# Differential attention's score products: 32-row fp32 matmuls replaced by one pass over stacked high and low parts

## The chip, the cores and the metric

The kernel runs on one core of one Trainium2 chip. The metric is the device time of one execution in microseconds (us), from the first to the last instruction with what lies around them; lower is better. The core has a matrix engine (PE, with its weight loads listed apart as PEld), a vector engine (DVE), a scalar engine (ACT), GpSimd (POOL) and SyncE (SP), which issues most of the DMAs. Each engine works through its own queue in order and waits on semaphores for the others.

## The reference

Two layers of an encoder for 256 tokens of width 1024. Each layer has token mixing (three head groups side by side), cross-attention into 256 memory tokens, and a gated feed-forward part with a short convolution. The change touches group C of the mixing, differential attention with 4 heads, each with two pairs of queries and keys of 32 values:

```python
def diff_group(dq, dk, dv, lam, lam_init, g_sub, cos, sin):
    q = partial_rope(dq.reshape(b, s, DIFF_HEADS, 2, DIFF_QK_DIM), cos, sin, 2 * DIFF_ROT)
    k = partial_rope(dk.reshape(b, s, DIFF_HEADS, 2, DIFF_QK_DIM), cos, sin, 2 * DIFF_ROT)
    v = dv.reshape(b, s, DIFF_HEADS, DIFF_V_DIM)
    scale = DIFF_QK_DIM ** -0.5
    def block(qb):
        sc = jnp.einsum('bqhcd,bkhcd->bhcqk', qb, k).astype(jnp.float32) * scale
        p = jax.nn.softmax(sc, axis=-1)
        a = (p[:, :, 0] - lam * p[:, :, 1]).astype(v.dtype)
        return jnp.einsum('bhqk,bkhe->bqhe', a, v)
```

So there are 8 score products per layer (4 heads by 2), each of 256 queries by 256 keys over 32 values.

## The kernel before

All large products are made with split operands: a float32 matrix is cut into a high part in the type fp32r, written by ACT, and a low part, the remainder, written by DVE (function `split`, lines 139 and 140; for weights with a gain lines 262 and 263). A product is then three fp32r matmuls, high by high, high by low and low by high (`mm_nat`, lines 270, 272 and 274; `mm_T`, lines 277 to 279). Weights stream in through `wunit`: a DMA into one of 6 raw buffers, then the split into one of 6 pairs. Plain float32 matmuls are used for transposes, for attention weights times values, and for the scores of the mixing groups (lines 638 and 770).

The mixing stage of a layer is a list of short steps written by hand (`MIX`, one string per layer). A step traces its instructions; a planner then orders the queue of each engine by the place in the trace and by what is ready, with costs of its own, so that instructions of neighbouring steps are interleaved. Only SyncE's queue stands as written.

The steps that matter here: `dL` and `dM0`/`dM1` make the projection for queries and keys of group C. `dn0`/`dn1` (`diff_qk`) copy one block of 128 tokens out of PSUM with its row factor on ACT and rotate it on DVE. `dT0`/`dT1` (`diff_qk_T`) transpose the block on PE and copy it to the tile `dT`, queries and keys apart, both on ACT. `s0` to `s3` (`diff_scores`) make the scores of a head, two PSUM banks of 2 blocks each, and call `softmax_exp` (row maximum on DVE, line 471; exponentials on ACT, line 475). `t` turns the probabilities, `w` multiplies them with the values. Around them stand `vL`/`vM` (values of group C, weights of 256 columns), `uL`/`wL`, `q`, `Q`, `kv`, `K`, `a`, `b`, `v`, `o` (group A), `zu`, `zv`, `sgu`, `ws`, `sg` (group B), `ms`, `mf`, `mg` (normalising, transposing and scaling the memory tokens, layer 0 only), and `pl`/`p`, pieces of the memory's keys and values that run in the single PSUM bank `fil`.

A score product before is two matmuls, one for each block of queries, on 32 of the 128 rows of PE's array; `tile_position` picks which rows. DVE's `rstd` chains pass through POOL (lines 159 and 178). The pool `t4` has 16 buffers of 4 KB a partition; `dT` takes one.

Of the kernel before, what the change touches and what calls it, by code (L numbers as in the profile page):

```python
# [13 lines left out]
F32 = mybir.dt.float32  # L14
F32R = mybir.dt.float32r
I32 = mybir.dt.int32
AF = mybir.ActivationFunctionType
ALU = mybir.AluOpType
# [3 lines left out]
P = 128  # L22
D = 1024
S = 256
# [11 lines left out]
H_C, QK_C, V_C, ROT_C = 4, 32, 64, 16  # L36
# [14 lines left out]

MIX = (
# [7 lines left out]
MEM = (  # L60
# [5 lines left out]
    "uL cw uM0 e0 uM1 e1")  # L66
BUFS = {"t4": 16, "t2": 10, "raw": 6, "w": 6, "acc": 4, "att": 3, "fil": 1, "gB": 2}

ENG = {"mrow": "A", "mT": "V", "dval": "A", "dn": "A", "dTq": "A", "dTk": "A", "kT": "A", "kn": "V",
    "va": "A", "qn": "A", "qT": "A", "mq": "A", "mo": "V", "up": "A", "ws": "A", "pt": "A"}  # L70
BANK = {"pd": "att", "po0": "acc", "po1": "acc", "tp": "att", "sc": "acc", "xs": "att", "xo": "att"}

# [2 lines left out]
def encoder(ctx, tc, a, out):  # L75
    nc = tc.nc
    V, A_, G, T = nc.vector, nc.scalar, nc.gpsimd, nc.tensor
# [9 lines left out]
    def nm(s):  # L87
        uid[0] += 1
        return f"{s}_{uid[0]}"

    def t4(dt=F32):
        return act.tile([P, UNIT], dt, tag="t4", bufs=BUFS["t4"], name=nm("t4"))

    def t2(dt=F32):
        return act.tile([P, 512], dt, tag="t2", bufs=BUFS["t2"], name=nm("t2"))
# [4 lines left out]
    def psum1(tag="att"):  # L100
        return pp.tile([P, 512], F32, tag=tag, bufs=BUFS[tag], name=nm(tag))

    def small(n, tag, bufs=4):
        return sm.tile([P, n], F32, tag=tag, bufs=bufs, name=nm(tag))
# [12 lines left out]
    mT = const.tile([P, KD, S], F32, name="mT")  # L117
# [20 lines left out]
    def split(h, lo, src):  # L138
        return (A_.activation(h, src, AF.Copy),  # L139
                V.tensor_tensor(lo, src, h.bitcast(F32), op=ALU.subtract))  # L140

    def copy(at, dst, src, scale=None):
        if ENG[at] == "A":
            A_.activation(dst, src, AF.Copy, scale=1.0 if scale is None else scale)
        elif scale is None:
            V.tensor_copy(dst, src)
        else:
            V.tensor_scalar(dst, src, scale, None, op0=ALU.mult)
# [94 lines left out]
    def group_T(src, kt):  # L243
        ps = psum1()
        pv = ps.rearrange("p (k b t) -> p k b t", k=2, b=NB)
        for b in range(NB):
            for k in range(2):
                T.transpose(pv[:, k, b, :], src[:, b, blk(k)], ident)
        split(hTH[:, kt:kt + 2, :], hTL[:, kt:kt + 2, :], ps.rearrange("p (k t) -> p k t", k=2))
# [31 lines left out]
    def blk(b):  # L281
        return slice(b * P, (b + 1) * P)
# [83 lines left out]
    def rope(out_v, src, n, rot, cs, sn):  # L366
        hf = rot // 2
        ta = sm.tile([P, 256], F32, tag="ropeA", bufs=1, name=nm("ropeA"))[:, :n * rot].rearrange("p (n r) -> p n r", r=rot)
        tb = sm.tile([P, 256], F32, tag="ropeB", bufs=1, name=nm("ropeB"))[:, :n * rot].rearrange("p (n r) -> p n r", r=rot)
        V.tensor_tensor(ta, src, cs.unsqueeze(1).broadcast_to([P, n, rot]), op=ALU.mult)  # L370
        V.tensor_tensor(tb[:, :, :hf], src[:, :, hf:], sn[:, :hf].unsqueeze(1).broadcast_to([P, n, hf]), op=ALU.mult)
        V.tensor_tensor(tb[:, :, hf:], src[:, :, :hf], sn[:, hf:].unsqueeze(1).broadcast_to([P, n, hf]), op=ALU.mult)  # L372
        V.tensor_tensor(out_v, ta, tb, op=ALU.add)
# [94 lines left out]
    def softmax_exp(acc):  # L468
        sv = acc.rearrange("p (b k) -> p b k", b=NB)
        nmx = small(NB, "nmax", 4)  # L470
        V.tensor_reduce(nmx, sv, axis=AX.X, op=ALU.max, negate=True)
        e = t2().rearrange("p (b k) -> p b k", k=S)
        ssum = small(NB, "psum", 10)
        for b in range(NB):
            A_.activation(e[:, b, :], sv[:, b, :], AF.Exp, bias=nmx[:, b:b + 1], accum_out=ssum[:, b:b + 1])
        return e, ssum
# [33 lines left out]
    for l in range(DEPTH):  # L510
# [3 lines left out]
        if l == 0:  # L514
# [5 lines left out]
            rr = []  # L520
        gm = pre_cols[:, l * KD:(l + 1) * KD]

        st = SimpleNamespace(units={}, e={}, t={}, flip={}, kr=[None] * NB, qn=[None] * NB, kn=[None] * NB)
        steps = mem.steps()
# [81 lines left out]

        def diff_qk(b):
            st.dn[b] = dn = t2()
            copy("dn", dn, st.d[b], rr[b])
            dv_ = dn.rearrange("p (n d) -> p n d", d=QK_C)  # L610
            rope(dv_[:, :, :ROT_C], dv_[:, :, :ROT_C], 16, ROT_C, cosD[:, b, :], sinD[:, b, :])

        def diff_qk_T(b):
            if b == 0:
                st.dT = t4().rearrange("p (k t) -> p k t", t=S)
            ps = psum1()
            for i in range(4):
                T.transpose(ps[:, blk(i)], st.dn[b][:, blk(i)], ident)
            pv = ps.rearrange("p (k t) -> p k t", t=P)
            copy("dTq", st.dT[:, 0:2, blk(b)], pv[:, 0:2, :], QK_C ** -0.5)  # L620
            copy("dTk", st.dT[:, 2:4, blk(b)], pv[:, 2:4, :])

        def diff_values():
            steps["vM_"]()
# [4 lines left out]
        def diff_scores(h):  # L629
            if h == 0:  # L630
                st.sd = small(NB * H_C, "s0s", 3).rearrange("p (b h) -> p b h", b=NB)
            es = []
            for c in range(2):
                acc = psum1(BANK["sc"])
                g = 2 * h + c
                rows = slice((g % 4) * QK_C, (g % 4 + 1) * QK_C)
                for b in range(NB):
                    T.matmul(acc[:, b * S:(b + 1) * S], st.dT[rows, g // 4, blk(b)], st.dT[rows, 2 + g // 4, :],  # L638
                             start=True, stop=True, tile_position=((g % 4) * QK_C, 0))
                es.append(softmax_exp(acc))  # L640
            (e0, s0), (e1, s1) = es
            V.tensor_copy(st.sd[:, :, h], s0)
            cf = small(NB, "cf", 2)
            V.reciprocal(cf, s1)
            V.scalar_tensor_tensor(cf, cf, nlam, s0, op0=ALU.mult, op1=ALU.mult)
            for b in range(NB):
                V.scalar_tensor_tensor(e0[:, b, :], e1[:, b, :], cf[:, b:b + 1], e0[:, b, :], op0=ALU.mult, op1=ALU.add)
            st.e["d", h] = e0
# [27 lines left out]
                V.tensor_tensor(ov, ov, st.gsc.unsqueeze(1).broadcast_to([P, H_C, V_C]), op=ALU.mult)  # L676

        steps["vM_"] = steps["vM"]
        steps.update(vM=diff_values, do=diff_out, gd=lambda: group_T(st.oc.rearrange("p b h d -> p b (h d)"), 6))
        for b in range(NB):  # L680
            steps[f"dn{b}"] = partial(diff_qk, b)
            steps[f"dT{b}"] = partial(diff_qk_T, b)
        for h in range(H_C):
            steps[f"s{h}"] = partial(diff_scores, h)
            steps[f"t{h}"] = partial(turn, ("d", h))
            steps[f"w{h}"] = partial(diff_v, h)
# [132 lines left out]
        rr = []  # L819
# [7 lines left out]
        steps = {"pl": mem.piece_load, "p": mem.piece}  # L827
        if l + 1 < DEPTH:
            steps = {**mems[l + 1].steps(), **steps}
# [67 lines left out]
        steps = mems[l + 1].steps() if l + 1 < DEPTH else {}  # L897
# [28 lines left out]
        for j in range(0, NF, 2):  # L926
# [4 lines left out]
            for s_ in range(2):  # L931
                if j < 4 and s_ == 0:
                    srcs = [first[j // 2][:, m * S:(m + 1) * S] for m in range(2)]
                else:
# [5 lines left out]
                    for m, acc in enumerate(accs()):  # L940
                        for kt in range(KD):
                            wH, wL = us[kt // 4]
# [16 lines left out]
        rr = [] if l + 1 < DEPTH else None  # L959
# [26 lines left out]
```

## Time and profile before

| what | value |
|---|---|
| time, median of 3 runs | 851.68 us (850.91 to 852.28) |
| profiled execution, its own time | 851.3 us |
| its span, first to last instruction | 849.5 us |
| PE busy | 833.2 us, 98% |
| DVE busy | 625.5 us, 74% |
| ACT busy | 546.9 us, 64% |
| POOL busy | 39.1 us, 5% |
| mean granted clock of PE | 0.997 of full speed |

The busy time of PE counts matmuls whose pipelines overlap, so the duration of one instruction is longer than the distance to the next one. What an instruction costs PE is read from the distance between starts. The chain of waits lists exactly that: each piece there lasts until the next piece of the chain takes over.

### The profile page before, as it was taken

To read this page: it belongs to the slowest core of one execution; us is meant where nothing else is said; L and a number is where in the kernel's file an instruction comes from. 1 tells how busy PE (TensorE), PEld (TensorE's weight loads), DVE (VectorE), ACT (ScalarE), POOL (GpSimd) and SP (SyncE) were. 2 spreads that over 40 slices of the span, in tenths; PEclk is the share of its full clock that TensorE was granted. 3 is DMA by queue.
4 is the path that set the end of the run, shared out by engine and by line. 5 is a ranking of instruction groups with operands and counts; after the bars stand their busy time and mean duration, and the time that the engine had idled before them with its cause. 6 is when DMAs were issued, how large, how long until landed. Compare 5 with 4: busy or idle time off the path is not lost.

```text
span 849.5 us, 13117 instructions
## 1 busy us (share of the span) xinstructions
PE 833.2 (98%) x4846; PEld 728.4 (86%) x4846; DVE 625.5 (74%) x1127; ACT 546.9 (64%) x1027; POOL 39.1 (5%) x65
## 2 busy tenths in 40 slices
PE   7999999999999999999999999999998999999997
PEld 5898999889888888888889989988996888888885
DVE  6798664776488999974487787548566799999543
ACT  7798663766368777763376777547636587777331
POOL 1120000100020000000010100001001000000000
PEclk9999999999999999999999999999999999999999
DMA  7873533572355667655737723256624446775531
GB/s 276 275 228 104 166 100 100 156 251 90 94 160 173 201 208 212 203 173 193 219 116 216 236 82 124 76 148 219 191 62 148 154 148 199 223 218 184 183 109 50
DMA packets 94704, 141.64 MB, mean 167 GB/s; under 512 B 5806, under 2 KB 71172, under 8 KB 94640
## 3 DMA queue, kind: packets, MB, share of 16 engines
q1 hardware_dynamic: 94368, 140.59, 52.8%
q8 instruction: 38, 0.62, 0.3%
q14 instruction: 26, 0.21, 0.1%
q0 software_dynamic: 160, 0.18, 0.1%
q10 hardware_dynamic: 112, 0.03, 0.0%
HBM read 139.74 MB, written 1.05 MB: 166 GB/s over the span
## 4 chain that ended last, share of the span: by engine, by line
PE 91%; DVE 4%; POOL 1%; issue 1%; DMA 1%; ACT 1%; SPq 0%; DVEq 0%; POOLq 0%; ACTq 0%
PE acc L943 18%; PE acc L270 13%; PE acc L272 13%; PE acc L274 13%; PE acc L944 9%; PE fil L270 2%; PE fil L274 2%; PE fil L272 2%; PE fil L277 2%; PE att L484 2%; PE fil L278 2%; PE fil L279 2%; PE acc L770 2%; PE acc L782 2%; PE acc L638 1%; PE att L204 1%
## 5 line engine op out<-in xcount | busy, mean ns | idle before, releaser
L140 DVE TENSOR_TENSOR wl<-raw,wh 128x1024 fp32r<-128x1024 f32 (+1 forms) x206 | 249.7, 1215 | 119.9 <-ACT wh L139 118.2
L139 ACT ACTIVATE wh<-raw 128x1024 fp32r<-128x1024 f32 (+1 forms) x206 | 215.6, 1051 | 129.6 <-PE acc L274 85.8
L943 PE MATMUL acc<-hT,wh 128*128 128x512 f32 x640 | 224.3, 396 | 0.0
L944 PE MATMUL acc<-hT,wl 128*128 128x256 f32 x640 | 178.8, 279 | 0.0
L943 PEld LDWEIGHTS acc<-hT,wh 128*128 128x128 f32 x640 | 120.2, 188 | 28.7
L272 PE MATMUL acc<-wl,hT 128*128 128x512 f32 (+3 forms) x384 | 134.9, 373 | 0.0
L274 PE MATMUL acc<-wh,hT 128*128 128x512 f32 (+3 forms) x384 | 134.4, 372 | 0.3 <-DVE hT L140 0.3
L270 PE MATMUL acc<-wh,hT 128*128 128x512 f32 (+3 forms) x384 | 134.7, 375 | 0.0
L944 PEld LDWEIGHTS acc<-hT,wl 128*128 128x128 f32 x640 | 120.7, 189 | 0.0
L274 PEld LDWEIGHTS acc<-wh,hT 128*128 128x128 f32 x384 | 72.7, 190 | 12.2 <-DVE hT L140 1.4
L272 PEld LDWEIGHTS acc<-wl,hT 128*128 128x128 f32 x384 | 72.6, 190 | 11.8 <-DVE wl L140 0.7
L270 PEld LDWEIGHTS acc<-wh,hT 128*128 128x128 f32 x384 | 72.3, 190 | 11.4 <-ACT hT L139 0.4
L270 PE MATMUL acc<-wh,t 128*128 128x512 f32 (+1 forms) x216 | 67.7, 387 | 0.0
L272 PE MATMUL acc<-wl,t 128*128 128x512 f32 (+1 forms) x216 | 67.5, 386 | 0.0
L274 PE MATMUL acc<-wh,t 128*128 128x512 f32 (+1 forms) x216 | 67.0, 384 | 0.0
L950 ACT ACTIVATE t<-t,cw 128x256 f32<-128x256 f32 x80 | 47.5, 595 | 13.9 <-DVE t L946 13.4
L262 ACT ACTIVATE wh<-raw,pre_cols 128x512 fp32r<-128x512 f32 (+3 forms) x80 | 43.7, 616 | 11.9 <-PE acc L274 7.8
L263 DVE SCALAR_TENSOR_TENSOR wl<-raw,pre_cols,wh 128x512 fp32r<-128x512 f32 (+3 forms) x80 | 46.1, 621 | 4.5 <-ACT wh L262 4.5
L270 PEld LDWEIGHTS acc<-wh,t 128*128 128x128 f32 x216 | 39.9, 188 | 8.2 <-issue 0.7
L274 PEld LDWEIGHTS acc<-wh,t 128*128 128x128 f32 x216 | 40.4, 188 | 7.5
L272 PEld LDWEIGHTS acc<-wl,t 128*128 128x128 f32 x216 | 40.3, 188 | 7.6 <-DVE ropeB L372 0.3
L178 POOL TENSOR_TENSOR rstd<-ms,nhalf 128x1 f32<-128x1 f32 x18 | 14.7, 819 | 605.0 <-DVE ms L176 600.4
(189 smaller groups left out, 1397.8 us busy)
## 6 DMA issues: line engine op xcount, KB each, us to landing
raw<-in_ffn_w_up SPq DMA_DIRECT2D x88, 512.0 KB, 4.6
raw<-in_ffn_w_down SPq DMA_DIRECT2D x44, 512.0 KB, 3.4
raw<-in_mem_w_kv SPq DMA_DIRECT2D x32, 512.0 KB, 3.7
raw<-in_w_in SPq DMA_DIRECT2D x20, 512.0 KB, 4.8
raw<-in_w_mix_out SPq DMA_DIRECT2D x16, 512.0 KB, 3.4
raw<-in_mem_w_q SPq DMA_DIRECT2D x16, 512.0 KB, 3.9
raw<-in_mem_w_o SPq DMA_DIRECT2D x16, 512.0 KB, 4.3
raw<-in_w_in SPq DMA_DIRECT2D x8, 384.0 KB, 4.6
```

The costliest lines, as they stand in the source:

```text
L139: return (A_.activation(h, src, AF.Copy), V.tensor_tensor(lo, src, h.bitcast(F32), op=ALU.subtract))
L140: V.tensor_tensor(lo, src, h.bitcast(F32), op=ALU.subtract))
L262: A_.activation(h[:, v], raw[:, v], AF.Copy, scale=g[:, i:i + 1])
L263: V.scalar_tensor_tensor(lo[:, v], raw[:, v], g[:, i:i + 1], h[:, v].bitcast(F32), op0=ALU.mult, op1=ALU.subtract)
L270: T.matmul(o, sH, w, start=start, stop=False)
L272: T.matmul(o, sH, w, start=False, stop=False)
L274: T.matmul(o, sL, w, start=False, stop=stop)
L277: T.matmul(o, wH, sH, start=start, stop=False)
L278: T.matmul(o, wH, sL, start=False, stop=False)
L943: T.matmul(acc, wH[:, kt % 4, blk(m)], hT[:, kt, :, :], start=kt == 0, stop=False)
L944: T.matmul(acc[:, :S], wL[:, kt % 4, blk(m)], hTH[:, kt, :], start=False, stop=kt == KD - 1)
L950: A_.activation(cv[:, m, :], src, AF.Identity, bias=cw[:, 3, f:f + 1], scale=cw[:, 1, f:f + 1])
```

## The change

Queries and keys of group C are cut into high (H) and low (L) parts and stacked: for each of the 8 score products, 96 rows hold H, H, L of the queries and H, L, H of the keys. One fp32r matmul over 96 rows then gives HH + HL + LH. The stacking copies between partitions are a step of their own, `dS`, placed right behind `dT1` in both lists. The scale of the queries moves into `diff_qk`.

```diff
-    "dT1 vL ms0 ms1 kF1 vM mf0 mf1 kF0 mg0 uL s0 q0 sg s1 q1 Q0 mg1 wL kv0 p s3 t0 Q1 w0 t1 pl s2 kv1 pg K0 "
+    "dT1 dS vL ms0 ms1 kF1 vM mf0 mf1 kF0 mg0 uL s0 q0 sg s1 q1 Q0 mg1 wL kv0 p s3 t0 Q1 w0 t1 pl s2 kv1 pg K0 "
-    "dL con dM0 dn0 zL dM1 zM cL cM dn1 pl kL dT0 p zu zv sgu dT1 ws cn0 vL cn1 kM cF0 kn0 uL kn1 vM sg kF0 "
+    "dL con dM0 dn0 zL dM1 zM cL cM dn1 pl kL dT0 p zu zv sgu dT1 dS ws cn0 vL cn1 kM cF0 kn0 uL kn1 vM sg kF0 "
         def diff_qk(b):
             st.dn[b] = dn = t2()
-            copy("dn", dn, st.d[b], rr[b])
+            qs = small(1, "qs", 2)
+            V.tensor_scalar(qs, rr[b], QK_C ** -0.5, None, op0=ALU.mult)
+            copy("dn", dn[:, :256], st.d[b][:, :256], qs)
+            copy("dn", dn[:, 256:], st.d[b][:, 256:], rr[b])
         def diff_qk_T(b):
             if b == 0:
-                st.dT = t4().rearrange("p (k t) -> p k t", t=S)
+                st.dH, st.dL = [t4(F32R).rearrange("p (k t) -> p k t", t=S) for _ in range(2)]
-            pv = ps.rearrange("p (k t) -> p k t", t=P)
-            copy("dTq", st.dT[:, 0:2, blk(b)], pv[:, 0:2, :], QK_C ** -0.5)
-            copy("dTk", st.dT[:, 2:4, blk(b)], pv[:, 2:4, :])
+            split(st.dH[:, :, blk(b)], st.dL[:, :, blk(b)], ps.rearrange("p (k t) -> p k t", t=P))
+        def diff_stack():
+            st.dS = [t4(F32R)[:3 * QK_C, :].rearrange("p (k t) -> p k t", t=S) for _ in range(4)]
+            q, k = slice(0, 2), slice(2, 4)
+            for r, to in enumerate(st.dS):
+                H, L = (t[r * QK_C:(r + 1) * QK_C, :, :] for t in (st.dH, st.dL))
+                one, two, three = (to[i * QK_C:(i + 1) * QK_C, :, :] for i in range(3))
+                V.tensor_copy(one, H.bitcast(F32))
+                A_.activation(two[:, q, :], H[:, q, :].bitcast(F32), AF.Copy)
+                V.tensor_copy(two[:, k, :], L[:, k, :].bitcast(F32))
+                G.tensor_copy(three[:, q, :], L[:, q, :].bitcast(F32))
+                A_.activation(three[:, k, :], H[:, k, :].bitcast(F32), AF.Copy)
         def diff_scores(h):
-                rows = slice((g % 4) * QK_C, (g % 4 + 1) * QK_C)
+                qk = st.dS[g % 4]
                 for b in range(NB):
-                    T.matmul(acc[:, b * S:(b + 1) * S], st.dT[rows, g // 4, blk(b)], st.dT[rows, 2 + g // 4, :],
-                             start=True, stop=True, tile_position=((g % 4) * QK_C, 0))
+                    T.matmul(acc[:, b * S:(b + 1) * S], qk[:, g // 4, blk(b)], qk[:, 2 + g // 4, :], start=True, stop=True)
```

## Rows read from the trace of the kernel before

**Rows 1.** The page's head, busy times, and the chain by engine.
```profile
span 849.5 us, 13117 instructions
...
PE 833.2 (98%) x4846; PEld 728.4 (86%) x4846; DVE 625.5 (74%) x1127; ACT 546.9 (64%) x1027; POOL 39.1 (5%) x65
...
PE 91%; DVE 4%; POOL 1%; issue 1%; DMA 1%; ACT 1%; SPq 0%; DVEq 0%; POOLq 0%; ACTq 0%
```

**Rows 2.** Busy time by stretch, layer 0 (first three) and layer 1; columns in the first line.
```profile
core 0: us, PE busy (x) PEld busy (x) DVE busy (x) ACT busy (x) POOL busy (x), PEclk, DMA share, GB/s
...
51.00:57.00 6.00, 6.00 (x47) 5.42 (x46) 6.00 (x24) 5.75 (x14) 2.75 (x3) 1.00 0.44 147
57.00:79.00 22.00, 21.47 (x125) 17.87 (x124) 19.39 (x55) 17.83 (x43) 0.42 (x1) 1.00 0.48 152
79.00:92.00 13.00, 13.00 (x98) 11.59 (x97) 11.83 (x24) 11.83 (x32) 0.00 (x0) 1.00 0.52 164
...
468.00:484.00 16.00, 16.00 (x130) 15.86 (x129) 11.64 (x33) 12.43 (x28) 2.83 (x4) 1.00 0.78 251
484.00:500.00 16.00, 16.00 (x107) 13.68 (x106) 14.26 (x41) 12.46 (x34) 0.00 (x0) 1.00 0.32 104
```

**Rows 3.** Groups by form: count, busy us, mean ns of one, idle before.
```profile
L277 PE MATMUL fil<-t,wh 128*128 128x256 f32 x128 | 38.3, 300 | 0.0
...
L638 PE MATMUL acc<-t 32*128 32x256 f32 x64 | 14.2, 405 | 0.0
...
L140 DVE TENSOR_TENSOR t<-att,t 128x512 fp32r<-128x512 f32 x16 | 10.5, 687 | 2.6 <-ACT t L139 2.6
```

**Rows 4.** Chain of waits, 30 to 120 us (layer 0): shares, then start, length, piece.
```profile
by line: PE fil L278 8.9%; PE fil L277 8.9%; PE fil L279 8.5%; DVE wl L263 8.3%; PE acc L638 6.4%; PE acc L770 5.8%; PE acc L272 5.4%; PE acc L274 5.1%; PE acc L270 5.1%; POOL rstd L159 4.3%; issue 3.9%; PE att L484 3.8%; PE att L661 3.6%; 
...
59.74 0.62 PE acc L638 x2
...
64.75 1.58 PE acc L638 x7
...
67.12 0.12 PE fil L279
...
84.89 1.07 PE acc L638 x8
...
99.26 1.30 PE acc L770 x6
```

**Rows 5.** Chain of waits, 390 to 530 us (layer 1).
```profile
by line: PE acc L274 23.3%; PE acc L272 23.3%; PE acc L270 23.2%; PE acc L638 4.5%; PE acc L770 4.4%; PE fil L277 3.4%; PE fil L279 3.0%; PE fil L278 3.0%; PE att L661 2.4%; PE att L484 2.3%; PE att L734 1.3%; PE att L760 1.3%; PE att L204 
...
485.89 1.07 PE acc L638 x8
486.96 0.55 PE acc L270 x2
...
487.87 0.35 PE acc L274 x2
```

**Rows 6.** DVE in order of time, layer 0: start, length; idle before in brackets.
```profile
69.40 1.22 DVE L140 TENSOR_TENSOR wl<-raw,wh 128x1024 fp32r<-128x1024 f32 x1
...
75.69 0.30 DVE L748 COPY t<-kr 128x256 f32<-128x256 f32 x1
75.89 0.76 DVE L146 COPY t<-acc 128x256 f32<-128x256 f32 x2
```

**Rows 7.** ACT in order of time, layer 0.
```profile
51.38 0.68 ACT L174 ACTIVATE t<-t 128x512 f32<-128x512 f32 x1
51.90 0.25 ACT L174 ACTIVATION_READ_ACCUMULATOR t<-t 128x1 f32 x1
```

**Rows 8.** POOL in order of time, layer 0.
```profile
1.55 0.29 POOL masks.py:199 TENSOR_SCALAR_AFFINE_SELECT ident<-ident 128x128 f32<-128x128 f32 x1
...
44.84 1.46 POOL L159 TENSOR_TENSOR rstd<-ms,nhalf 128x1 f32<-128x1 f32 x1 [2.23 <-DVE ms L157]
50.32 0.55 POOL L159 TENSOR_TENSOR rstd<-ms,nhalf 128x1 f32<-128x1 f32 x1 [4.02 <-DVE ms L157]
```

More of the change, by code (lines that the diff above doesn't have):

```diff
@@ L67 @@
 BUFS = {"t4": 16, "t2": 10, "raw": 6, "w": 6, "acc": 4, "att": 3, "fil": 1, "gB": 2}
-ENG = {"mrow": "A", "mT": "V", "dval": "A", "dn": "A", "dTq": "A", "dTk": "A", "kT": "A", "kn": "V",
+ENG = {"mrow": "A", "mT": "V", "dval": "A", "dn": "A", "kT": "A", "kn": "V",
     "va": "A", "qn": "A", "qT": "A", "mq": "A", "mo": "V", "up": "A", "ws": "A", "pt": "A"}
@@ L678, in encoder @@
         steps["vM_"] = steps["vM"]
-        steps.update(vM=diff_values, do=diff_out, gd=lambda: group_T(st.oc.rearrange("p b h d -> p b (h d)"), 6))
+        steps.update(vM=diff_values, dS=diff_stack, do=diff_out, gd=lambda: group_T(st.oc.rearrange("p b h d -> p b (h d)"), 6))
         for b in range(NB):
```

## Prediction

> **What bounds the kernel now.** I read the page's head first: PE is busy 98% of the span and the chain that ended last is 91% PE [rows 1]. So time taken off PE is worth its full length wherever PE never waits, and the other engines cost nothing as long as they stay ahead of it. Whether they do has to be read by stage. In the mixing stage of layer 1 they do: from 468 to 484 us DVE is busy 11.64 and ACT 12.43 of 16 us [rows 2], and the chain from 390 to 530 us is PE in all its large shares [rows 5]. In layer 0 they don't: the chain from 30 to 120 us has DVE's weight remainders (L263) with 8.3% and POOL's L159 with 4.3% among the matmuls [rows 4]. From 51 to 57 us DVE is busy 6.00 of 6.00 us and ACT 5.75, while PE is full too [rows 2]. There PE and DVE finish together: weights arrive just in time. It is in that stretch that the new step stands, right behind the second transpose. The question is thus what each layer gives, and they must be priced apart.
>
> **What PE gains.** A score product before is two calls, and the group of the score line counts 64 matmuls for 32 calls, so each fp32 call is run as two instructions [rows 3]. On the chain the score line takes 6.4% of 90 us = 5.8 us in layer 0 [rows 4]; the first six of its 32 instructions lie before the chain comes to PE, and for them I add 1.0, since eight in a row take 1.07, so 6.8 us. In layer 1 it takes 4.5% of 140 = 6.3 us [rows 5]. Behind a group the next matmul comes late: the first pair of L270 takes 0.55 us where a later pair takes 0.35 [rows 5], 0.2 us more; with six groups in a layer, smaller where a short matmul follows, I add 0.8 us. Before: 7.6 us in layer 0, 7.1 in layer 1.
>
> After, 16 calls a layer stand there as fp32r matmuls of 256 columns, one instruction each. The trace has no such matmul on 96 rows. The nearest rows are the fp32r matmul on 128 rows, 0.12 us from start to start [rows 4], and the plain fp32 pass on 96 rows, 1.30 us for six = 0.217 us, with no delay behind it [rows 4]. The lower gives 16 x 0.12 = 1.9 us, the upper 3.5 us. I take the lower, since columns and type are the same and rows don't show in the price. The gain on PE is then 5.7 us in layer 0 and 5.2 in layer 1 (4.1 and 3.6 by the upper).
>
> The Trainium skill, page TensorEngine Tiling (Array Packing), section Key Properties, speaks against giving up the 32-row tiles: different tiles load and multiply in parallel. The trace agrees in part: eight instructions in a row take 1.07 us, 0.13 each, where two alone take 0.62 [rows 4]. If every group ran as densely, the scores before would cost 32 x 0.13 = 4.3 us a layer and the gain would be 2.4; the chain's own shares decide, and they say 6.8 and 6.3 us.
>
> **What the other engines pay, in each layer.**
> DVE: the low part of two transposed blocks, 2 x 0.69 us [rows 3], where DVE did nothing before: 1.4. Two tiny scalings, by my estimate from the 0.2 us between the start of the 256-element copy and its follower, at most 0.2 together [rows 6]. Eight copies in SBUF, four of 1024 and four of 512 elements a partition. The nearest row is L748, 256 elements in 0.20 us from start to start, against 0.38 each for the same size out of PSUM (L146) [rows 6]: SBUF copies go at about twice the pace. At 0.20 for each 256 that is 4 x (0.8 + 0.4) = 4.8 us, and less if a part of the 0.20 is fixed: 3.6 if a quarter of the total is. Above: the price of a two-input op, 1.22 us for 1024 [rows 6], 4 x (1.22 + 0.61) = 7.3. I take 4.3, nearer to L748's pace than to its lower end, because these copies change partitions each time and the overlap of neighbours (0.1 us behind L748) may be lost. Sum: 5.9 us; bounds 5.2 and 8.9.
> ACT: eight copies of 512 elements at 0.52 us from start to start [rows 7] = 4.2 us. `dn` in two halves adds about 0.2; one `split` high part for two copies of half the size changes nothing. Sum 4.4.
> POOL: four copies of 512. The only row with a tile is 128 elements in 0.29 us [rows 8]: between 0.29 and 4 x 0.29 = 1.17 each, 1.2 to 4.7 us, beside a POOL that is idle most of the stage. I take 1.0 each, off the path.
> No DMA is added or moved. `dS` takes four buffers of `t4` until `s2` and `s3` where `dT` took one; counted from the list some 17 are then wanted for 16 at the first `p` of layer 0, whose copy out of `fil` may have to wait for `s3` or `Q1`. I set that at nothing, since these stand next to it; if not, it holds `fil` for about a microsecond.
>
> **Layer 1.** DVE's idle time from 468 to 484 us is 16 - 11.64 = 4.4 us, ACT's 3.6, and from 484 to 500 another 1.7 and 3.5 [rows 2]. So 5.9 and 4.4 us fit before 500 us, and PE, which has pieces of `fil` and weights in hand, does not notice more than some 0.2 us: gain 5.0.
>
> **Layer 0.** The new work stands in front of `vL`, `ms` and `uL` in DVE's and ACT's queues, in a stretch where DVE has no idle time at all. Behind it wait the last remainders of the value weights, then the memory's normalising, the weights of `q` and the rest; PE waits for each in turn. So all that PE does up to the end of DVE's full stretch moves by 5.9 us less what DVE idles until 79 us, 22 - 19.39 = 2.6 [rows 2]: 3.3 us late. PE's own gain before 79 us is lost, for PE waits there anyway. What is left of it: the group at 84.89 us, 1.07 less 0.5, and part of the one before, 0.62 less 0.24 [rows 4], 1.0 us. From 92 us on PE is the bound again. Net 2.3 us lost.
>
> **Sum.** 2.3 - 5.0 = -2.7 us on the profiled execution's 851.3, so 848.6. The median of the runs is 0.4 above the profiled one: 849.0.
>
> **Rivals.**
> (A) The cover holds in layer 0 too. For it: the planner orders by what is ready and may pull `fil` pieces or transposes forward, and ACT and DVE have gaps after 57 us. Against it: DVE full from 51 to 57. Then both gains count, 5.7 + 5.2 = 10.9: 840.8.
> (B) Slower: DVE and POOL get in each other's way in `dS`. For it: POOL's same 128x1 op takes 0.55 us at 50.32 and 1.46 at 44.84, when DVE runs a 1024-element remainder [rows 8]. Place: the four POOL copies between DVE's eight. If DVE stands for 1.0 us at each, it pays 9.9 us; layer 0 loses 9.9 - 2.6 - 1.0 = 6.3, layer 1 gains about 3.5 (9.9 less the 6.1 of idle time to 500 us leaves 3.8, of which perhaps half reaches PE): 851.7 + 2.8 = 854.5. The copies at DVE's full price, 8.9, give nearly the same. It decides the sign from about 8.6 us of added DVE work.
> The rule behind it stands in the Trainium skill, page SBUF — State Buffer, section Who interferes with whom: VectorE and GpSimd share one port pair as an exclusive lock, and a copy inside SBUF in its two-port pace takes it. The trace's 0.55 against 1.46 us agrees.
> (C) The two effects cancel: layer 0 loses 5 us, by 2 us of waits between engines in `dS` (every row of the stack needs three engines, and `s0` needs its last). Time 851.7.
> (D) It doesn't do what it says: the new matmul still runs as two instructions of 0.217 us. Then 32 x 0.217 = 6.9 us stand against 7.6 and 7.1, layer 1 gains 0.2, layer 0 still comes 3.3 late, and the time is 854.8. Against it: `fil` counts 128 for its 128 calls [rows 3].
>
> **How the numbers follow.** My forecast 0.42, (A) 0.24, (B) 0.20, (C) 0.11, (D) 0.03. I forecast 849.0. A measurement of this kernel can tell about 0.2%, 1.7 us, from no change. The forecast's own range is 846 to 851: 2 up by the dearer matmul (1.6 in layer 1, 0.4 behind 79 us), 3 down if `fil` pieces fill PE's wait in layer 0 entirely. Together: (A) and nine tenths of the forecast are faster, 0.62; (C) and the rest of the forecast, with a few of (B), the same, 0.17; (B) and (D) slower, 0.21. The range runs from 842, a gain in layer 0 all but complete, to 855, the slower cases' price.
>
> **What would show it.** The score line should count 32, each about 0.28 us long with 0.12 between starts, and its share of the chain fall to some 2 us a layer. DVE's busy time should rise by about 12 us, ACT's by 9, POOL's by 8. PE should wait between 52 and 79 us in layer 0, 3 to 6 us in all, for DVE or ACT, and nowhere in layer 1 around 468 to 500. I am wrong if PE stays full in layer 0 (A), if the 1024-element copies take over 1 us or POOL's rows stretch beside them (B), or if the score line counts 64 (D).

## The result and the profile after

The changed kernel takes 859.37 us (median of 4 runs, 858.22 to 860.32) against 851.5 for the kernel before on the same chip: ratio 1.0091, 95% interval 1.0078 to 1.0104. It is 7.9 us slower, where 2.7 us faster was forecast, and lies above the range.

The page of the changed kernel, head, busy times and chain by engine [rows 1]:

```profile
span 858.0 us, 13102 instructions
...
PE 830.2 (97%) x4814; PEld 728.5 (85%) x4814; DVE 638.9 (74%) x1151; ACT 557.0 (65%) x1043; POOL 44.6 (5%) x73
...
PE 82%; DVE 4%; ACT 3%; issue 1%; POOL 1%; DVEq 0%; POOLq 0%; ACTq 0%
```

PE has 32 instructions and 3.0 us of busy time less, DVE 13.4, ACT 10.1 and POOL 5.5 us more, where 12, 9 and 8 were forecast. But the span grew by 8.5 us. Groups by form of the changed kernel [rows 3]:

```profile
L140 DVE TENSOR_TENSOR t<-att,t 128x512 fp32r<-128x512 f32 x20 | 13.3, 686 | 2.8 <-ACT t L139 2.8
L653 PE MATMUL acc<-t 96*128 96x256 f32 x32 | 7.7, 332 | 3.5 <-DVE t L634 2.7 <-ACT t L475 0.6
L635 POOL CAST t<-t 32x512 fp32r<-32x512 f32 x8 | 6.2, 771 | 5.9 <-DVE t L140 4.7 <-DVE kr L373 0.9
L632 DVE CAST t<-t 32x1024 fp32r<-32x1024 f32 x8 | 6.1, 766 | 0.1
...
L634 DVE CAST t<-t 32x512 fp32r<-32x512 f32 x8 | 4.3, 539 | 0.1
```

The product (L653) is one instruction for each call, 32 in all, as forecast. The splits cost DVE 686 ns each, four more than before. What differs is where PE waits. Windows of the changed kernel, four stretches of [rows 2] and two short ones:

```profile
51.00:57.00 6.00, 3.31 (x26) 2.90 (x25) 5.52 (x22) 5.91 (x15) 3.04 (x5) 1.00 0.63 179
57.00:79.00 22.00, 17.92 (x105) 16.81 (x106) 20.25 (x48) 16.70 (x34) 4.43 (x4) 0.77 0.46 144
...
468.00:484.00 16.00, 16.00 (x121) 15.83 (x120) 13.38 (x25) 11.70 (x24) 5.57 (x6) 1.00 0.52 165
484.00:500.00 16.00, 13.37 (x92) 13.17 (x91) 14.51 (x42) 10.46 (x22) 2.58 (x4) 0.89 0.64 193
...
64.00:66.00 2.00, 2.00 (x12) 2.00 (x11) 2.00 (x3) 1.15 (x1) 2.00 (x2) 0.50 0.71 233
...
492.00:494.00 2.00, 2.00 (x11) 2.00 (x11) 2.00 (x6) 1.06 (x1) 0.00 (x0) 0.51 0.59 164
```

PE was full in these stretches before, but for half a microsecond. Now it is idle for 6.8 of 28 us from 51 to 79, and for 2.6 us from 484 to 500, in layer 1, where no wait was forecast. Behind each hole the granted clock is 0.50, the 1.2 GHz level, though PE is busy again; below this is called the half clock. What it waited for (engine, line, releaser: us in total, times, longest), layer 0 and then layer 1:

```profile
PE acc L653 <- DVE t L634: 2.7, 2, 1.8
PE acc L272 <- DVE wl L263: 1.9, 1, 1.9
PE att L186 <- DVE t L712: 1.7, 1, 1.7
...
PE acc L270 <- DVE t L712: 2.6, 1, 2.6
```

Not only the scores wait for the copies (L634): in layer 0 the value product (`vM`) waits for weight remainders (L263), and the transposes L186 wait for the normed latents (L712). In layer 1 the value product waits for L712 too, but not for its result. It stops in front of its 13th matmul, the first of the second block of tokens; the weights for it had just served the first 12, and by the code the accumulator bank that it wants next (`acc` has 4) is the one that L712 reads last. The chain in layer 1 shows what made L712 late (start, length, piece):

```profile
478.40 1.00 DVE t L632
479.41 0.74 DVE t L634
...
485.12 2.85 DVE wl L263 x7
487.98 0.14 DVE ms L157 x2
488.12 1.08 POOL rstd L159 x2
489.22 0.16 DVE rstd L167
489.38 0.54 DVE t L712
...
490.35 0.12 PE acc L272
490.72 0.21 PE acc L272
```

It goes from the copies to the weight remainders, to the latents' norm through POOL and back to DVE, and to PE; [rows 5] had PE alone there. The last two rows show the same matmul at 0.12 and, once the clock is down, 0.21 us.

A ruler for what follows: a layer's length is taken in PE's timeline, from the start of the first transpose of group C's queries and keys to the start of the last product of group A's probabilities with its values; waits are PE's gaps in it. Each length is of one profiled execution.

| kernel | layer 0 (waits) | layer 1 (waits) | time |
|---|---|---|---|
| before | 100.2 (0.5) | 87.9 (0.0) | 851.5 to 852.0 |
| changed | 105.4 (7.7) | 89.9 (3.4) | 859.4 |

The layers lost 5.1 and 2.0 us. The rest of the 7.9 is 0.8 us between the two layers (below); the 0.6 to 1.9 us by which layer 0 starts later in the profiles show in kernels with an untouched layer 0 too.

### The profile page after: what moved, and what is told of

It is laid out like the page before. It is cut to its first block, busy times and chain, and to the rows that moved or that the text cites. A ratio compares the mean times of both kernels' runs of the same rounds, so it can differ in the third digit from the quotient of the medians.

```text
span 858.0 us, 13102 instructions
## 1 busy us (share of the span) xinstructions
PE 830.2 (97%) x4814; PEld 728.5 (85%) x4814; DVE 638.9 (74%) x1151; ACT 557.0 (65%) x1043; POOL 44.6 (5%) x73
## 4 chain that ended last, share of the span: by engine, by line
PE 82%; DVE 4%; ACT 3%; issue 1%; POOL 1%; DVEq 0%; POOLq 0%; ACTq 0%
PE acc L957 17%; PE acc L270 12%; PE acc L272 11%; PE acc L274 11%; PE acc L958 9%; PE fil L270 2%; PE fil L274 2%; PE fil L272 2%; PE acc L784 2%; PE att L484 2%; PE acc L796 2%; PE fil L277 1%; PE fil L279 1%; PE fil L278 1%; PE att L204 1%
## 5 line engine op out<-in xcount | busy, mean ns | idle before, releaser
L140 DVE TENSOR_TENSOR wl<-raw,wh 128x1024 fp32r<-128x1024 f32 (+1 forms) x206 | 249.3, 1214 | 118.2 <-ACT wh L139 117.0
L270 PE MATMUL acc<-wh,hT 128*128 128x512 f32 (+3 forms) x384 | 136.2, 379 | 2.6 <-DVE t L712 2.6
L274 PE MATMUL acc<-wh,hT 128*128 128x512 f32 (+3 forms) x384 | 136.0, 376 | 0.6 <-DVE hT L140 0.6
L272 PEld LDWEIGHTS acc<-wl,hT 128*128 128x128 f32 x384 | 74.4, 194 | 14.1 <-DVE wl L263 2.2
L270 PEld LDWEIGHTS acc<-wh,hT 128*128 128x128 f32 x384 | 73.8, 194 | 14.0 <-DVE t L712 2.8
L274 PEld LDWEIGHTS acc<-wh,hT 128*128 128x128 f32 x384 | 74.4, 194 | 12.8 <-DVE hT L140 1.9
L964 ACT ACTIVATE t<-t,cw 128x256 f32<-128x256 f32 x80 | 47.5, 595 | 13.8 <-DVE t L960 13.4
L263 DVE SCALAR_TENSOR_TENSOR wl<-raw,pre_cols,wh 128x512 fp32r<-128x512 f32 (+3 forms) x80 | 45.9, 620 | 5.7 <-ACT wh L262 5.7
```

Of the source, the lines that this page charges most:

```text
L263: V.scalar_tensor_tensor(lo[:, v], raw[:, v], g[:, i:i + 1], h[:, v].bitcast(F32), op0=ALU.mult, op1=ALU.subtract)
L270: T.matmul(o, sH, w, start=start, stop=False)
L272: T.matmul(o, sH, w, start=False, stop=False)
L274: T.matmul(o, sL, w, start=False, stop=stop)
L964: A_.activation(cv[:, m, :], src, AF.Identity, bias=cw[:, 3, f:f + 1], scale=cw[:, 1, f:f + 1])
```

## The experiments

Four theories were put against each other. T1: the place; the copies stand ahead of the next products' weight splits in the queues. T2: DVE and POOL hinder each other in the step. T3: DVE and ACT have no room for the added work, wherever it stands. T4, formed later for layer 1: DVE's amount of work makes it the bound there.

**Taking the change apart.** The product without copies (e2, and e2r, the same kernel run again for its profile) replaces the body of the step by one line:

```diff
+            st.dS = [st.dH[:3 * QK_C, :, :]] * 4
```

The copies without the product (e3) compute the scores from the high parts by the old product; the split alone (e7) has both edits:

```diff
-                qk = st.dS[g % 4]
+                rows, dT = slice((g % 4) * QK_C, (g % 4 + 1) * QK_C), st.dH.bitcast(F32)
...
-                    T.matmul(acc[:, b * S:(b + 1) * S], qk[:, g // 4, blk(b)], qk[:, 2 + g // 4, :], start=True, stop=True)
+                    T.matmul(acc[:, b * S:(b + 1) * S], dT[rows, g // 4, blk(b)], dT[rows, 2 + g // 4, :],
+                             start=True, stop=True, tile_position=((g % 4) * QK_C, 0))
```

> The new score product with no stacking copies: it reads 96 rows of the transposed high parts as they are, so the low parts of the scores and the right pairing of the rows are left out; split and scalings stay. What the product alone gives. By the prediction's term (7.6 and 7.1 us before, 1.9 after, per layer) PE gains 10.9 us: 841, at most 843 with the 1.6 us more that the split's low parts and the scalings cost DVE in layer 0. If the prediction's upper price for the 96-row product holds (0.217 us each), 844 to 846. If the gain on PE is not real and waits elsewhere take its place, 849 or more.

> The kernel without stacking copies again (scores of 96 unpaired rows of high parts, low parts left out), for a profile of an undisturbed execution. The score line should take about 2.7 us a layer from start to start instead of 6.8 and 6.4, as in layer 1 of the runs with the stack moved or without POOL; PE should wait about 2 us in layer 0 (the latent queries behind the split's low part on DVE) and nowhere in layer 1: 847 to 850.

> The old 32-row float32 score product on the transposed high parts (the low parts left out of the scores), with split, scalings and all stacking copies made but read by nobody. What the added work alone costs. If gain and cost are independent, this is 859.4 less 841 above the kernel before: 868 to 871. If the cost is only delay that the old product would partly have hidden (PE busy on scores while copies run), 858 to 866. If the added work costs nothing by itself, and the new product's dependence on the last copy is what hurts, 851 to 854.

> The old 32-row float32 product on the transposed high parts (the low parts are left out of the scores), with the split and the two scalings, and without any stacking copies. What the split alone costs, so that the product's gain (run without copies) and the copies' price (run with unused copies) can be read as differences. By the prediction's term DVE has 1.6 us more in each layer, hidden in layer 1 and not in layer 0: 852.5 to 854; if it stands in front of the latent weights in layer 0 and moves PE's later waits too, 854 to 857; if hidden in both layers, 851.5 to 852.5.

| kernel | layer 0 (waits) | layer 1 (waits) | time | ratio, interval |
|---|---|---|---|---|
| split only (e7) | 104.4 (2.3) | 87.9 (0.0) | 856.6 | 1.0062, 1.0047 to 1.0077 |
| split, product (e2; layers from e2r) | 102.2 (5.2) | 83.2 (0.2) | 848.7 | 0.9955, 0.9941 to 0.9968 |
| split, copies (e3) | 109.9 (6.4) | 96.3 (3.3) | 867.6 | 1.0188, 1.0167 to 1.0209 |

In layer 1 the split is free, the product gives 4.7 us, and the copies take 6.7 (83.2 to 89.9). In layer 0 the split alone takes 4.1, the product gives 2.2 back, the copies take 3.2. (Of the 8.4 us between e7 and e3 in layer 1 about 2.9 are no cost: 24 more matmuls of the memory's pieces, 0.12 each, fell into that layer. With the old product the copies so cost 5.5 us in each layer: costs and gains don't simply add.) PE's waits in layer 0 of e2r, without any copies:

```profile
PE acc L270 <- DVE ropeB L372: 1.9, 1, 1.9
PE att L413 <- ACT t L144: 1.5, 2, 0.9
PE att L186 <- DVE t L703: 1.5, 1, 1.5
```

Two low parts, 1.4 us of DVE, are enough there for waits in three places: DVE had no room from 51 to 57 us [rows 2], and PE, made shorter, only waits longer. In e2r the half clock adds to it: 36 matmuls of the latent queries take 9.4 us (waits taken out) instead of 6.5. Behind such a wait e7, too, falls to half clock (its windows):

```profile
73.00:75.00 2.00, 2.00 (x8) 1.88 (x8) 1.55 (x8) 1.75 (x8) 0.00 (x0) 0.50 0.07 17
```

Without POOL (e4), its copies are made by DVE:

```diff
-                G.tensor_copy(three[:, q, :], L[:, q, :].bitcast(F32))
+                V.tensor_copy(three[:, q, :], L[:, q, :].bitcast(F32))
```

> The four stack copies of each layer that POOL did are done by DVE instead, so DVE has about 1.7 to 2 us more of its own work in each layer and nothing of POOL's runs beside the step. T2: the stretched DVE copies (0.73 instead of 0.42 us, 1.0 instead of 0.7) fall back to their short form, and the time falls by 2 us or more below 859. T1: the place is the cause, DVE's extra work costs about what POOL's cost, 858 to 862. T3: more work on DVE, 861 to 864.

e4: 860.43 us, ratio 1.0097 (1.0061 to 1.0133), its executions between 856.4 and 863.7: no different from the change within this spread. The hindrance is real: in the changed kernel copies on DVE are stretched beside POOL's (DVE in order of time):

```profile
477.64 0.74 DVE L634 CAST t<-t 32x512 fp32r<-32x512 f32 x1
...
481.19 0.42 DVE L634 CAST t<-t 32x512 fp32r<-32x512 f32 x1
```

POOL's four copies, in one row, cover the first and not the second:

```profile
477.17 3.46 POOL L635 CAST t<-t 32x512 fp32r<-32x512 f32 x4 [4.66 <-DVE t L140]
```

In e4 all take their short form, 0.42 and 0.68 us. But four times 0.32 us is 1.3, and POOL's four copies cost DVE 4 x 0.42 = 1.7. Layer 1 fell to 87.0, layer 0 rose to 108.3, in a profiled execution 3.3 us above its median; 1.5 us of the fall are the value product at full clock (6.1 us instead of 7.6). The median says that gain and cost about cancel. The Trainium skill, page SBUF — State Buffer, section Who interferes with whom, says that a DVE copy in its two-port pace and GpSimd shut each other out; the 0.42 against 0.74 us agree that they hinder each other. T2 as the main cause is not borne out: it wanted 2 us or more back. How much of the loss is the 1.3 us of stretch, e4 can't say, since it trades the stretch for more work on DVE.

**Moving the copies.** First the step goes right ahead of the first scores in both lists (e1):

```diff
-    "dT1 dS vL ms0 ms1 kF1 vM mf0 mf1 kF0 mg0 uL s0 q0 sg s1 q1 Q0 mg1 wL kv0 p s3 t0 Q1 w0 t1 pl s2 kv1 pg K0 "
+    "dT1 vL ms0 ms1 kF1 vM mf0 mf1 kF0 mg0 uL dS s0 q0 sg s1 q1 Q0 mg1 wL kv0 p s3 t0 Q1 w0 t1 pl s2 kv1 pg K0 "
...
-    "dL con dM0 dn0 zL dM1 zM cL cM dn1 pl kL dT0 p zu zv sgu dT1 dS ws cn0 vL cn1 kM cF0 kn0 uL kn1 vM sg kF0 "
-    "s0 q0 s1 cF1 pg ... "
+    "dL con dM0 dn0 zL dM1 zM cL cM dn1 pl kL dT0 p zu zv sgu dT1 ws cn0 vL cn1 kM cF0 kn0 uL kn1 vM sg kF0 "
+    "dS s0 q0 s1 cF1 pg ... "
```

> The stacking step stands right ahead of the first score step in both layers, everything else as in the changed kernel. Theory T1 (place in the queues): the stack copies stood ahead of the weight splits of the next products on ACT and DVE, and PE ran dry behind them. Then PE's waits near 55 to 62 us and near 490 us go, the stretches granted 0.50 behind them too, and the time falls from 859 to between 840 and 850. Theory T2 (DVE and POOL hinder each other inside the step): the copies are as slow here as there, DVE loses the same time, and the time stays above 855. Theory T3 (there is simply more work on DVE and ACT than the mixing stage has room for, wherever it stands): 853 to 860.

856.58 us, ratio 1.0055 (1.004 to 1.007): 3 us won, and far from the 840 to 850 of T1. Layer 0 stays at 105.5 (7.2), layer 1 falls to 87.2 (3.0). PE's waits, layer 0 and layer 1:

```profile
PE acc L653 <- DVE t L634: 2.2, 2, 1.5
PE acc L270 <- DVE ropeB L372: 2.0, 1, 2.0
PE att L186 <- DVE t L712: 1.7, 1, 1.7
...
PE fil L279 <- DVE wl L140: 1.6, 1, 1.6
PE att L484 <- DVE t L661: 0.8, 1, 0.8
```

The waits have moved with the copies. T1 holds for at most a third of the loss; T3, which said 853 to 860, fits the rest. And of the 2.7 us that layer 1 fell, the waits are only 0.4 and the value product 1.7: it ran at full clock in e1's profiled execution. Whether that comes with the place is not shown.

Then DMAs make the stack: from SyncE at that late place (e6), and from ACT's queue at the place of the change (e8, with `nc.scalar`). One of five lines:

```diff
-                V.tensor_copy(one, H.bitcast(F32))
+                nc.sync.dma_start(one.bitcast(F32), H.bitcast(F32))
```

> The stack is made by 20 DMAs a layer from SyncE's queue, placed right ahead of the first score step, instead of copies on DVE, ACT and POOL; everything else as in the changed kernel. It takes 4.6 us of DVE's and 5.1 us of ACT's work out of each layer (0.68 + 0.42 and 2 x 0.63 us for each of four row groups, read in the trace of the run with the late stack) and leaves the split's low parts and the scalings. Theory T3, as it now stands (DVE and ACT have no room for the copies in layer 0, wherever they stand, and little in layer 1): PE's waits go, the time comes near that of the product alone (848.7), 847 to 852. Rival: the scores now wait for the DMAs (1.6 MB a layer, several us behind the last low part), or the weights queue behind them on SyncE: 853 to 862, with PE waiting on a DMA at the first score group.

> The stack by DMAs from ACT's queue at the place where the changed kernel has the step. If issuing a DMA holds ACT for little, it lands earlier than from SyncE ahead of the scores, and the time is 847 to 852 (T3); if each issue waits for DVE's low part and holds back ACT's splits of the value weights behind it, PE starves as in the changed kernel: 854 to 860.

e6: 858.96 us, ratio 1.0086 (1.0069 to 1.0103); layers 103.3 (7.9) and 94.0 (4.1), the latter with the same 24 matmuls, 2.9 us, that e3 had more in it. e8: 871.0, ratio 1.0226 (1.0211 to 1.0241); layers 111.4 (13.4) and 96.0 (9.1). The rival's times came. In e6 PE waits for no DMA, the sign that was named, but it holds that the weights queue behind the copies. SyncE's queue in e6:

```profile
53.05 0.60 SPq L632 DMA_DIRECT2D t<-t  x1
...
66.25 0.59 SPq L636 DMA_DIRECT2D t<-t  x1
67.28 0.81 SPq L254 DMA_DIRECT2D raw<-in_mla_w_ukv  x2
```

Each issue takes 0.59 us of the queue, 20 of them 13 us, and the weights' loads stand behind: those of L254 above start at 67.28 us, in the kernel before at 47.70. On ACT (e8) its own work stands behind the issues, and PE waits 13.4 us in layer 0, 3.0 of them for a DMA.

**Layer 1 alone.** Layer 0 keeps the old product from here on (100.2 us in each), since in e2r even without copies it lost 2 us.

In e9 the stack comes in two halves on the engines of the change, in e11 POOL makes 12 of the copies early (dSp) and DVE's stand in those halves; the list of layer 1, its first line for e11 alone, its second for both:

```diff
+    "... sgu dT1 dSp ws cn0 vL cn1 kM cF0 kn0 uL kn1 vM sg kF0 "
+    "dSa s0 q0 dSb s1 cF1 pg ... "
```

In e10 the step stands where the change has it, and in e10 to e12 POOL makes ACT's copies too (one of two lines):

```diff
-                A_.activation(two[:, q, :], H[:, q, :].bitcast(F32), AF.Copy)
+                G.tensor_copy(two[:, q, :], H[:, q, :])
```

e12 is e11 with dSp behind cn1; e14 has the whole step behind cn1, e15 to e17 right ahead of s0. All from e12 on have the scaling on POOL:

```diff
-            V.tensor_scalar(qs, rr[b], QK_C ** -0.5, None, op0=ALU.mult)
+            G.tensor_scalar(qs, rr[b], QK_C ** -0.5, None, op0=ALU.mult)
```

In e16 ACT makes `two[:, k, :]` and POOL `three[:, k, :]`, so DVE has only `one`. In e17 the split writes crosswise, low queries and high keys into X, the others into Y:

```diff
+                nc.sync.dma_start(two.bitcast(F32), Y)
+                nc.sync.dma_start(three.bitcast(F32), X)
+                A_.activation(one[:, q, :], Y[:, q, :], AF.Copy)
+                A_.activation(one[:, k, :], X[:, k, :], AF.Copy)
```

> Layer 0 as in the kernel before. In layer 1 the changed product, with the stack made in two halves on the same engines: row groups 0 and 1 right ahead of the first score step, 2 and 3 ahead of the second. Layer 0 then keeps its 100.2 us. If the late step of layer 1 cost what it did (87.15 us for the layer against 83.2 without copies and 87.9 before) because half of it stood needlessly ahead of other work, the layer falls to 84 to 86 us and the kernel to 848.5 to 850.5. If the whole amount of DVE's and ACT's work counts (4.6 and 5.1 us), wherever it stands, the layer stays at 87 and the time at 850.5 to 852.

> Layer 0 as in the kernel before. In layer 1 the stack at the place of the changed kernel, but ACT's eight copies are done by POOL, 12 copies there. In the changed kernel's trace ACT makes its weight splits for the values (L262 x8) only after its copies, 5 us later than before, and PE runs dry behind that. If ACT's copies are the cause there, the layer falls from 89.9 to 84 to 86 us and the time is 848 to 850.5. If it is DVE's copies (4.6 us, stretched by POOL's beside them to 6 or 7), the layer stays at 88 to 90 and the time at 852 to 854.5.

> Layer 0 as in the kernel before. In layer 1 POOL makes its 12 copies at the place of the changed kernel, early, and DVE's copies stand in halves ahead of the first and the second score step; ACT makes none. Only DVE's 4.4 us are left on a busy engine, at the place where they are wanted. If place and engine both matter, this is the best of the three, layer 1 at 84 to 85 us, 847.5 to 850. If POOL's copies hinder DVE's work in between (its copies went from 0.42 to 0.74 us beside POOL), the layer stays at 86 to 88, 850 to 853.

> The kernel of the run with both edits (layer 0 as before; in layer 1 POOL makes 12 copies early, DVE its copies in halves ahead of the score steps), with two edits more: POOL's copies stand behind the latent norms (cn0, cn1) instead of ahead of them, and the scaling of the row factor for the queries is done by POOL, not DVE. In that run POOL's power for the latents waited for its last copy (480.41 us) and PE waited 2.1 us behind that; the scaling made DVE wait 0.66 us for POOL, and PE came 0.8 us later into layer 1. If these two are what is left of the price, layer 1 falls from 88.1 to 85 to 86 us and the time from 852.8 to 848.5 to 850.5. If DVE's own work, stretched beside POOL's copies, is the price, it stays at 851 to 853.

> Layer 0 as before; in layer 1 the whole stack on the engines of the change, behind the splits of the value weights and the latent norms (between cn1 and kM), with the scaling on POOL. A place between the early one (layer 1 89.9 us; ACT's weight splits stood behind the copies) and the late one (87.2; the copies stood ahead of the scores and of what follows them). If the price is the queue's order, 85 to 86.5 us for the layer, 849 to 851. If any place costs 4 us, because DVE and ACT have to be fed all the time, 87 to 88 us and 851 to 853.

> Layer 0 as before; in layer 1 the whole stack late, right ahead of the first score step, on the engines of the change, with the scaling on POOL. In the run with both layers late this layer took 87.15 us against 87.89 before. If the layers add up, the kernel gains 0.7 us there and is not late at the layer's start: 850.5 to 851.5. Theory T4 (in the stretch from 466 to 510 us, where DVE was busy 35.3 of 44 us, the split's 1.4 and the copies' 4.4 us make 41.1, and PE needs only 44 less 4.7 = 39.3: DVE is the bound and no place helps): 87 us and no more than that gain.

> As the run beside it, but with DVE's part of the copies cut from 4.4 to 2.7 us: DVE makes only the four copies of 1024, ACT the eight copies of the second rows (5 us, as before), POOL eight copies of the third rows (5.6 us). T4: DVE's work in the stretch falls to 39.4 us, level with PE's 39.3, and the layer gains up to 1.7 us on the run beside it: 85.5 to 86.5 us, 849 to 850.5. If POOL's eight copies stretch DVE's work beside them by as much (0.3 us each was seen, 2.4 in all), nothing is gained: 851 to 852.5.

> Layer 0 as before; in layer 1 the late stack with no copy on DVE or POOL. The split writes its parts crosswise (one tile with the low queries and high keys, one with the high queries and low keys), so that each row group needs two whole DMAs from SyncE (8 a layer, 0.6 us of SyncE's queue each, 4.8 us) and two ACT copies of 512 (8, 5.0 us). The split becomes four instructions a block instead of two, about 0.4 us more on DVE and on ACT. T4 (DVE's amount is the price): DVE has 2.3 us less than in the run with 2.7 us of copies, and the layer falls from 86.3 to 84 to 85.5 us, 848 to 849.5. If the softmax chain of the scores, or SyncE's loads of the memory's weights held back behind the DMAs, sets the layer's length instead: 86 to 88 us, 850 to 852.

| kernel | layer 1 (waits) | time | ratio, interval |
|---|---|---|---|
| e9, late, halves | 89.1 (3.8) | 856.5 | 1.0044, 1.003 to 1.0057 |
| e10, early, no ACT | 89.9 (4.3) | 855.3 | 1.0039, 1.0026 to 1.0051 |
| e11, POOL early, DVE late | 88.1 (2.8) | 852.8 | 1.001, 1.0 to 1.002 |
| e12, POOL behind the norms | 88.2 (4.2) | 852.7 | 1.0005, 0.9996 to 1.0015 |
| e14, behind the value weights | 88.5 (3.5) | 852.9 | 1.001, 0.9999 to 1.0022 |
| e15, late | 87.0 (2.9) | 850.4 | 0.9981, 0.9972 to 0.999 |
| e16, late, less on DVE | 86.3 (2.6) | 850.1 | 0.9982, 0.9973 to 0.9991 |
| e17, late, none on DVE | 90.7 (4.3) | 855.1 | 1.004, 1.0026 to 1.0053 |

The half clock blurs this table. In the profiled executions of e10, e11, e14 and e17 a stretch of it lies in layer 1, in the other four none; in e10, e11 and e14 one product so takes 1.5 to 1.9 us longer than in e2r. Between the two sets 1 to 2 us can be the clock's. e9's profiled execution took 853.2 us at a mean granted clock of 0.998, 3.3 less than its median; of its twelve executions three, at 0.998 and 0.999, took about 853, the others, at 0.991 to 0.994, took 855.7 to 858.1.

Two theories of one culprit fell. ACT was suspected because its splits of the value weights come late in the changed kernel (ACT in order of time):

```profile
476.21 0.59 ACT L144 ACTIVATE t<-att 128x512 f32<-128x512 f32 x1
...
481.72 0.63 ACT L636 ACTIVATE t<-t 32x512 fp32r<-32x512 f32 x1
...
482.94 3.30 ACT L262 ACTIVATE wh<-raw,pre_cols 128x256 fp32r<-128x256 f32 x8
```

The same in e2r, which has no copies:

```profile
472.87 0.59 ACT L144 ACTIVATE t<-att 128x512 f32<-128x512 f32 x1
...
474.46 1.71 ACT L262 ACTIVATE wh<-raw,pre_cols 128x256 fp32r<-128x256 f32 x4
```

6.7 us behind L144 instead of 1.6. With ACT's copies on POOL (e10) the layer stays at 89.9: there the latents' power stands behind POOL's copies. In e11 too (POOL in order of time):

```profile
479.72 0.61 POOL L648 CAST t<-t 32x512 fp32r<-32x512 f32 x1
480.41 1.06 POOL L159 TENSOR_TENSOR rstd<-ms,nhalf 128x1 f32<-128x1 f32 x2
```

And DVE's wait for it there:

```profile
480.99 0.16 DVE L167 TENSOR_TENSOR rstd<-rstd,rrow 128x1 f32<-128x1 f32 x1 [1.79 <-POOL rstd L159]
```

Put behind the norms (e12) they let the power through, and PE waits elsewhere: 88.2. T4, DVE's amount, predicted e15 (87.0) and not quite half of the next step: 1.7 us less on DVE (e16) gave 0.7 in the layer and nothing clear of noise in the time. With no copies on DVE (e17) it failed; the scores then come late behind ACT's copies, in front of the softmax. PE's waits in e16:

```profile
PE acc L666 <- ACT t L475: 1.6, 1, 1.6
PE att L484 <- DVE t L674: 0.8, 1, 0.8
```

The chain in e17 (L645 is one line of ACT's copies, L475 the softmax with its table):

```profile
488.54 0.63 ACT t L645
...
490.08 1.28 ACT L475
491.38 1.94 ACT t L475 x8
```

Even with 2 us taken off for the clock e10 and e17 stay above what the two theories wanted, 84 to 86 and 84 to 85.5 us. So in the changed kernel and these eight, whichever engine makes them and at each place, the copies cost 3.1 to 7.4 us in layer 1 (over the 83.2 of e2r, the half clock included), where the product gives 4.7. The best two, e15 and e16, beat the kernel before by 0.2%.

Last, e13 is the changed kernel, both layers, with nothing but the scaling moved to POOL.

> The changed kernel with one edit: the scaling of the row factor (one value a row, two a layer) is done by POOL right behind its own power, not by DVE. If DVE's wait for POOL at the start of layer 1 is what brings PE 0.8 us late there, the step from 6.1 to 6.9 us behind the kernel before goes, and the time falls by 0.8 us, to 858.0 to 858.8. If PE was late for another reason, the time stays at 859.4.

858.64 us, ratio 1.0081 (1.0064 to 1.0098); the median is 0.7 us lower, where 0.8 was expected, but the intervals overlap: the time alone doesn't show it. The profiles do. The changed kernel's DVE ahead of layer 1:

```profile
438.65 0.20 DVE L176 TENSOR_SCALAR ms<-ss 128x1 f32<-128x1 f32 x1
439.52 0.15 DVE L610 TENSOR_SCALAR qs<-rrow 128x1 f32<-128x1 f32 x1 [0.66 <-POOL rrow L178]
```

One value a row, but it stands in DVE's queue ahead of the split of the layer's inputs and waits there for POOL. In the changed kernel PE was 6.1 us behind the kernel before at 434 us and 6.9 at layer 1's first transpose; in e13 it is 7.2 at both, and in all kernels with the scaling on POOL the step is gone: from the end of layer 0 to the start of layer 1 they take 323.4 us, as the kernel before, and all with it on DVE take 324.2 or 324.3.

e13 shows one thing more. Its layer 1 has the wait of the changed kernel, at the same place, but behind it the clock stays at full speed (waits, then windows of e13):

```profile
PE acc L270 <- DVE t L712: 2.6, 1, 2.6
...
490.00:492.00 2.00, 1.76 (x14) 1.77 (x15) 2.00 (x6) 1.56 (x5) 0.00 (x0) 1.00 0.66 221
```

Its value product takes 6.1 us (waits taken out) where the changed kernel's takes 7.6, and its layer 88.8 us against 89.9. The half clock is thus a cost of its own, which comes behind a wait in one execution and not in another.

## Why the prediction was wrong

**The step that failed** is the cover in layer 1: "5.9 and 4.4 us fit before 500 us, and PE ... does not notice more than some 0.2 us: gain 5.0". Without the copies it is nearly right: 4.7 gained (e2r). The copies took 6.7. The idle time that was added up, 4.4 us of DVE and 3.6 of ACT from 468 to 484 [rows 2], is there, but it isn't room. The weights and latents of the next products pass ACT, DVE, POOL, DVE and PE in turn, like a relay. Every copy in a queue delays one leg, and an engine's idle time can be its wait for another leg. And PE, 4.7 us shorter, is the less a cover. Shown: with the copies PE waits 2.6 to 4.3 us in layer 1 wherever they stand (9.1 in e8), for one piece or another of this relay (such as L712, L140, L167) or for the softmax (L475), and 0.2 without them. Left open: how much each leg gives, and what a freer accumulator bank would have given; no one engine's amount of work accounts for it.

**Layer 0**: the mechanism was right, DVE full and the next weights late, the size was not. Forecast 2.3 lost, measured 5.1. PE's waits grew by 7.1 us where 3.3 were forecast. The 2.6 us of DVE's idle time until 79 us were taken as room again, but 1.75 of them stayed idle. ACT's copies also stood in front of the memory's norms.

**The half clock** was in no term. Behind the waits the 48 matmuls of the value product take 8.3 us from start to start (waits taken out) instead of 6.3 in layer 0, and 7.6 instead of 5.8 in layer 1: 2.0 and 1.7 us on top of the waits, in this execution. So in layer 0 7.1 us of waits and 2.0 of slow matmuls stand against 3.2 of gain in the score line, in layer 1 3.4 and 1.7 against 3.6; the rest of the layers makes -0.9 and +0.5.

**The product's gain** was mis-sized. One instruction, 0.12 us apart, was right. But the score line takes 6.8 and 6.4 us before, not 7.6 and 7.1: the chain's shares already held the lateness behind groups that I added. And that lateness stays: 2.9 and 2.4 us in e2r, not 1.9. So 4.0 a layer in e2r, not 5.7 and 5.2; the other 0.7 of layer 1's 4.7 lies outside the score line.

**Prices of the copies** were nearly right: DVE 4.4 us a layer unstretched (4.3 forecast) and 5.2 beside POOL, ACT 5.0 (4.2), POOL 0.77 each (1.0). The scalings take 0.15 us each, where at most 0.2 together was said, and the wait of 0.66 in front of one was not looked for: 0.8 us of the kernel.

**The rivals.** (B) came nearest in size, by another mechanism than its own: its sign showed, two of four 1024-element copies take 1.00 and 1.01 us in layer 1, but the stretch is 1.3 us a layer where it took 4 (e4). Its threshold of 8.6 us also keeps layer 1's gain whole; with the half that (B) itself lets through to PE it is about 8. (C) had layer 0's loss, 5 us, but layer 1 as a gain. (A) and (D) are out: DVE had no cover in layer 0, and the line counts 32.

The sum as it came: 5.1 + 2.0 + 0.8 = 7.9 us.

## What to carry to other kernels

Idle time of an engine in a window is room only for work on which nothing in its queue waits; where products pass several engines in turn, price an insertion by what stands behind it in each queue. Price PE's wait with the slow stretch that can follow it. When an edit makes the bounding engine shorter, ask whether the others can still feed it: here at best (e16) a third of the product's gain was left in layer 1 (1.6 of 4.7 us), and none in layer 0.

## What the runs showed of the hardware that was not expected

- A DMA of 64 or 128 KB within SBUF takes 0.59 us of the issuing queue (e6, and 0.60 on ACT in e8), so 20 small ones are 13 us of issue, though each lands in about 2 us.
- A tiny operation on DVE costs what it waits: 0.15 us of work, 0.66 of wait on POOL's power of 0.55 us (changed kernel, 438.94 us).
- Behind PE's waits the granted clock can stay at 0.50, the 1.2 GHz level, for some microseconds of full work: a 256-column matmul every 0.21 us instead of 0.12 (changed kernel, layer 1). It need not: behind the same wait of 2.6 us it stayed at 1.00 in e13.
